# A transformer block on one core: gate rows in column groups, pool products in float32r passes, context keys with features on the partitions

## The chip, the cores and the metric

The kernel runs on one core of a Trainium2 chip. The metric is the time of one execution on the device in microseconds (us). The core has a TensorE (PE; its weight loads are shown apart as PEld), a VectorE (DVE), a ScalarE (ACT), a GpSimd (POOL) and a SyncE (SP), which here only issues transfers. All of them run side by side, each through its own list of instructions, and wait for one another on semaphores.

## What is computed

One layer of a diffusion backbone on 1024 latent tokens (a grid of 16 rows and 64 columns) and 256 context tokens, width 1024, in float32:

```
h_x = rmsnorm(x) * (1 + sc1) + sh1         # the same for the context, with its own shift and scale
u, q, k, v = split(h_x @ w_in)             # u: 512 wide for the pools; q, k, v: 8 heads of 64
pool:  y[g] = (window_mean(u[g], w) - u[g]) @ pool_w[g] * pool_scale     # 4 groups, w = 2, 4, 8, 16
attn:  softmax over an 8 x 16 neighbourhood (with a position bias) and all 256 context keys
x = x + gt1 * rmsnorm(concat(pool, attn) @ w_out)
x = x + gt2 * rmsnorm(relu(modulated(x) @ w_mlp_in) ** 2 @ w_mlp_out)
```

The shifts, scales and gates (sh, sc, gt) are six rows of `silu(c) @ w_mod + b_mod`, each 1024 long. Only the latent tokens are returned.

## The kernel before

**Number formats.** Most products are made of three float32r passes (helper `three`, L167 to L170): each operand is split into a high part (rounded to float32r) and a low part (the rest), and high x high, high x low and low x high are added up in PSUM. `split` (L142) makes the two parts: ScalarE casts the high one (L143), VectorE subtracts it from the source for the low one (L144). A few small products are plain float32 matmuls, which the trace shows as two records each: the sums of the modulation (L341), the gate rows (L198), the pools' products (L575), the scores (L669) and the weighted values (L745).

**Memory.** Large operands live in 33 equal pages of 128 x 1024 elements (`page`, pool "act", one tag). A page is given to a tile when its first instruction is issued, and goes back when the last instruction that reads it is done. Raw weights have 4 buffers (`wraw`), their high and low parts 8 (`whl`). During the projections PSUM has 6 banks for products (`ps1`) and 2 for lasting ones.

**Order.** In stretches marked `in_order` (the startup up to the context keys, the attention, the end of the MLP) each engine's instructions run in the order of the program. Elsewhere the framework that builds the kernel orders each engine's list: of the instructions whose inputs and buffers are free at that point, the one that stands first in the program is taken. The order is then fixed.

**The stages up to attention**, with what each leaves in pages:

1. Startup: tokens are normalised and transposed, `mod_rows` (L341) makes shift and scale with float32 products of 32 x 256 in four column groups of the array, keys kT are made for the latents (`some_keys`, L382). The modulated latents hx take 16 pages (2 blocks of 512 tokens, 8 k steps), kT takes 4.
2. Context keys (L494 to L517): `token_group` makes pkc, with tokens on the partitions, for two groups of 128 context tokens, 8 k steps of three passes of 512 columns each. ScalarE copies to kct; after each group of context values PE transposes four blocks of kct (L514) and ScalarE copies them to kcT, with the features on the partitions, which is what the scores need. The weights wv for the values take over the buffers of the key weights, and their splits stand after the second group (L501).
3. Values (pvc, pv; pages vc and v, 1 + 4). In between, VectorE does `background` steps: `mod_sum` (L190) adds 128 rows of w_mod at a time, weighted, into an accumulator of 128 x 1024 (accsh, accsc, acca, accb; b_mod is loaded into its first row). `mod_gate` (L193) sums an accumulator over the partitions, by a matmul with a matrix of ones, in two halves of 512 columns, and multiplies with the norm's gain; row 0 is stored to DRAM (L468) and read back as a page on all partitions when it is needed (L211): G1 near the end of attention, G2 in the MLP.
4. Pools (L581 to L588): for each of four groups, u is projected (two blocks of 512 tokens, pu), copied to a page u (L586), and `pooled` (L538) makes the window sums on VectorE in two pages sa and sb that take turns, then the difference from u; the page with the result is kept in dT.
5. Queries (L622): four groups for the first block of tokens, with background steps between them, the mask and the position tables (pages msk, U and four tab), one group for the second block, and `pool_out` (L571): one float32 product of 512 columns for each pool group and block, whose result is scaled and split into the page or raw buffer mix.
6. Attention, in 32 units, `in_order`: another query group, then for each unit scores, softmax, transposes and values. The last two query groups stand after the scores of units 0 and 1. VectorE adds the bias and takes the minimum (L683), ScalarE the exponential (L692).

After that come the output projection and the MLP (seven products in place of eight for each block, in `three` passes).

Of the kernel before, what the change touches and what calls it, by code (L numbers as in the profile page):

```python
# [10 lines left out]
F32 = mybir.dt.float32  # L11
F32R = mybir.dt.float32r
# [5 lines left out]
P = 128  # L18
D = 1024
KT = D // P  # L20
SEQ = 1024
NT = SEQ // P
CTX = 256
# [10 lines left out]
QR, QC = 16, 8  # L34
NM = GW // QC
# [44 lines left out]
def hybrid_block(ctx, tc, x, ctx_in, w_mod, b_mod, gp1, gp2, w_in, pool_w, rpb, w_out, w1, w2, vectors,  # L80
                 mask, edge, out):
    nc = tc.nc
    sub, mul, add = ALU.subtract, ALU.mult, ALU.add

    const = ctx.enter_context(tc.tile_pool(name="const", bufs=1))
    wraw = ctx.enter_context(tc.tile_pool(name="wraw", bufs=4))
# [11 lines left out]
    def page(name, dt=F32):  # L98
        return act.tile([P, 1024], dt, tag="pg", name=name)
# [21 lines left out]
    ident = cst("ident", [P, P])  # L121
    make_identity(nc, ident)
    ones = cst("ones", [P, P])
# [18 lines left out]
    def split(src, hi, lo):  # L142
        nc.scalar.copy(hi, src)  # L143
        nc.vector.tensor_tensor(lo, src, hi.bitcast(F32), sub)  # L144

    def load(name, src):
        raw = wraw.tile([P, 1024], F32, tag="raw", name=f"{name}w")
        nc.sync.dma_start(raw.rearrange("p (a b) -> p a b", b=src.shape[-1]), src)
        return raw
# [13 lines left out]
    def wk(w, k, lo, c, n):  # L163
        return w[k // 2][lo][:, (k % 2) * 512 + c : (k % 2) * 512 + c + n]


    def three(ps, ahi, alo, bhi, blo, first, last, more=False):  # L167
        nc.tensor.matmul(ps, ahi, bhi, start=first, stop=False, skip_group_check=more)  # L168
        nc.tensor.matmul(ps, ahi, blo, start=False, stop=False, skip_group_check=more)  # L169
        nc.tensor.matmul(ps, alo, bhi, start=False, stop=last, skip_group_check=more)  # L170
# [12 lines left out]
    def mod_sum(name, c, alloc, sT):  # L183
# [4 lines left out]
        for k in range(KT):  # L188
            w = load(f"wm{name}_{k}", w_mod[k * P : (k + 1) * P, c * D : (c + 1) * D])
            nc.vector.scalar_tensor_tensor(acc, w, sT[:, k : k + 1], acc, mul, add)  # L190
            yield acc

    def mod_gate(name, acc, gp, bank):  # L193
        g = load(f"gp{name}", gp.rearrange("(o d) -> o d", o=1).to_broadcast([P, D]).rearrange("p (a b) -> p a b", a=2))
        for h in range(2):
            hs = slice(h * 512, (h + 1) * 512)
            ps = bank(f"pg{name}{h}")
            nc.tensor.matmul(ps, ones, acc[:, hs], start=True, stop=True)  # L198
            nc.vector.tensor_tensor(acc[:, hs], ps, g[:, hs], mul)

    def mod_column(name, acc, bank):
        ps = bank(f"pc{name}")
# [4 lines left out]
    gates = {}  # L207
# [15 lines left out]
    with tc.tile_pool(name="ps1", bufs=6, space=PSUM) as ps1, tc.tile_pool(name="tmp1", bufs=3) as tmp:  # L223

        def bank(name):
            if name[:2] == "pm" or name in ("pxt0_6", "pxt0_7", "pxt1_6", "pxt1_7", "pct2", "pct3"):
                return lasting(name)
            return ps1.tile([P, 512], F32, tag="mm", name=name)

        def once(name, shape):  # L230
            return tmp.tile(shape, F32, tag=name, name=name, bufs=1)
# [141 lines left out]
        wgt = []  # L373
# [55 lines left out]
        for k in range(KT):  # L429
            for i in range(2):  # L430
                o = (k % 2) * 256 + i * P
                nc.tensor.transpose(pct[k // 2][:, o : o + P], cp[i][:, k * P : (k + 1) * P], ident)
        hc = []
        for k in range(KT):
            if k % 2 == 0:
                hp = page(f"hc{k}", F32R)
            o = (k % 2) * 512
# [23 lines left out]
        def mod_row(name, c, gp):  # L461
            for acc in mod_sum(name, c, page, sx):
                yield

            def close():
                mod_gate(name, acc, gp, bank)
                gates[name] = dram.tile([1, D], F32, tag=f"g{name}", name=f"g{name}")
                nc.sync.dma_start(gates[name], acc[0:1, :])  # L468

            closing.append(close)  # L470

# [14 lines left out]
        def token_group(ps, w, hk):  # L486
            for k in range(KT):
                hi, lo = hk(k)
                three(ps, hi, lo, wk(w, k, 0, 0, 512), wk(w, k, 1, 0, 512), k == 0, k == KT - 1)

        ctx_tok = lambda i: lambda k: (hc[k][0][:, i * P : (i + 1) * P], hc[k][1][:, i * P : (i + 1) * P])
        lat_tok = lambda b, i: lambda k: (hx[b][k][:, i * P : (i + 1) * P], hx[b][k][:, 512 + i * P : 512 + (i + 1) * P])

        kcp = page("kcT")  # L494
        kct = page("kct").rearrange("p (i f) -> p i f", i=2)
        raw_v = [load(f"wv{kk}", pair(w_in, kk, 1536, 512)) for kk in range(KT // 2)]
        for i in range(2):
            ps = bank(f"pkc{i}")
            token_group(ps, wgt, ctx_tok(i))
            if i:  # L500
                wgt = [high_low(f"wv{kk}", raw_v[kk]) for kk in range(KT // 2)]  # L501
            nc.scalar.copy(kct[:, i], ps)
        startup.close()
        with tc.issue_after(last[ET.DVE]):
            background(4)
# [1 line left out]
        for i in range(2):  # L507
            ps = bank(f"pvc{i}")
            token_group(ps, wgt, ctx_tok(i))
            nc.scalar.copy(vcp[:, i * 512 : (i + 1) * 512], ps)  # L510
            background()
            pt = bank(f"pkct{i}")
            for j in range(4):
                nc.tensor.transpose(pt[:, j * P : (j + 1) * P], kct[:, i, j * P : (j + 1) * P], ident)  # L514
            nc.scalar.copy(kcp.rearrange("p (j i t) -> p i j t", j=4, i=2)[:, i],
                               pt.rearrange("p (j t) -> p j t", j=4))
        kc = kcp.rearrange("p (j t) -> p j t", j=4)  # L517

        vp = [page(f"v{i}") for i in range(4)]
        for m in range(NM):  # L520
            ps = bank(f"pv{m}")
# [3 lines left out]
            if m == NM - 1:  # L525
                wgt = [high_low(f"wu{kk}", raw_u[kk]) for kk in range(KT // 2)]
# [4 lines left out]

        pwt = once("pwt", [P, 4, P])
        nc.sync.dma_start(pwt, pool_w.rearrange("g c d -> c g d"))
        edg = once("edg", [P, 4, 16])
        nc.sync.dma_start(edg, edge.rearrange("o (g e) -> o g e", g=4).to_broadcast([P, 4, 16]))
        dT = []

        def pooled(g, up):  # L538
            w = WINDOWS[g]
            lo, hi = w // 2, w - 1 - w // 2  # L540

            bufs = [page(f"sa{g}"), page(f"sb{g}")]
            cur, span, i = up, 1, 0
            while span < w:
                nxt = bufs[i % 2]
                i += 1
                n = SEQ - 2 * span + 1
                nc.vector.tensor_tensor(nxt[:, :n], cur[:, :n], cur[:, span : span + n], add)
                cur, span = nxt, 2 * span

            ed = tmp.tile([P, 16], F32, tag="ed", name=f"ed{g}", bufs=2)
            nc.vector.reduce_sum(ed[:, 0:1], up[:, 0 : hi + 1], axis=mybir.AxisListType.X)
            for q in range(1, lo):
                nc.vector.tensor_tensor(ed[:, q : q + 1], ed[:, q - 1 : q], up[:, hi + q : hi + q + 1], add)
            if hi:
                nc.vector.reduce_sum(ed[:, 7 + hi : 8 + hi], up[:, SEQ - 1 - lo : SEQ], axis=mybir.AxisListType.X)
            for q in range(hi - 2, -1, -1):
                t = SEQ - hi + q
                nc.vector.tensor_tensor(ed[:, 8 + q : 9 + q], ed[:, 9 + q : 10 + q], up[:, t - lo : t - lo + 1], add)
            dp = bufs[i % 2]  # L560
            nc.vector.scalar_tensor_tensor(dp[:, lo : SEQ - hi], cur[:, : SEQ - w + 1], 1.0 / w,
                                           up[:, lo : SEQ - hi], mul, sub)
            nc.vector.tensor_tensor(ed[:, :lo], ed[:, :lo], edg[:, g, :lo], mul)
            nc.vector.tensor_tensor(dp[:, :lo], ed[:, :lo], up[:, :lo], sub)
            if hi:
                nc.vector.tensor_tensor(ed[:, 8 : 8 + hi], ed[:, 8 : 8 + hi], edg[:, g, 8 : 8 + hi], mul)
                nc.vector.tensor_tensor(dp[:, SEQ - hi :], ed[:, 8 : 8 + hi], up[:, SEQ - hi :], sub)
            return dp


        def pool_out(g):  # L571
            dv = dT[g].rearrange("p (r m c) -> p m r c", r=QR, m=NM)
            for b in range(2):
                ps = bank(f"py{g}_{b}")
                nc.tensor.matmul(ps, pwt[:, g, :], dv[:, 4 * b : 4 * b + 4], start=True, stop=True)  # L575
                mp = page(f"mix1_{g}", F32R) if b else wraw.tile([P, 1024], F32R, tag="raw", name=f"mix0_{g}")
                nc.scalar.activation(mp[:, :512], ps, AF.Identity, scale=pscol[:, g : g + 1])
                nc.vector.scalar_tensor_tensor(mp[:, 512:], ps, pscol[:, g : g + 1], mp[:, :512].bitcast(F32), mul, sub)
                mix[b][g] = mp

        for g in range(4):  # L581
            up = page(f"u{g}")
            for b in range(2):
                ps = bank(f"pu{g}_{b}")
                feature_group(ps, wgt, g * P, b, range(KT))
                nc.scalar.copy(up.rearrange("p (r m c) -> p m r c", r=QR, m=NM)[:, 4 * b : 4 * b + 4],  # L586
                                   ps.rearrange("p (m r c) -> p m r c", m=4, r=QR))
            dT.append(pooled(g, up))  # L588


        tabs, msk = [], []
# [26 lines left out]
        wgt = in_group("wq", 512)  # L618
# [22 lines left out]
    with (  # L641
# [4 lines left out]
        bank = lasting  # L646
# [209 lines left out]
    with tc.tile_pool(name="ps2", bufs=6, space=PSUM) as ps2:  # L856
# [6 lines left out]
      with ExitStack() as tmp2:  # L863
        tmp = tmp2.enter_context(tc.tile_pool(name="tmp2", bufs=4))
# [342 lines left out]
        with tc.issue_after(first[ET.PE]), in_order(ET.PE, ET.Activation, ET.DVE, ET.SP):  # L1207
# [5 lines left out]
            tmp = tmp2.enter_context(tc.tile_pool(name="tmp3", bufs=4))  # L1213
# [138 lines left out]
```

## Time and profile before

| what | value |
|---|---|
| time, median of 3 runs | 1063.97 us (1063.96 to 1064.71) |
| the profiled execution | 1063.25 us |
| its span, first to last instruction | 1061.5 us |
| granted TensorE clock, mean | 0.997 |
| PE busy | 1045.0 us |
| VectorE / ScalarE busy | 685.6 / 506.8 us |
| context keys begin / values begin | 79.0 / 89.8 us |
| pools' projections | 148.9 to 192.4 us |
| first scores | 235.5 us |

How to read it: times in the trace are microseconds from the start of the span. A row of the timeline gives start, duration, engine, line, operation, output <- inputs, shape and count, and in brackets how long the engine was idle before and what it waited for. Buffer numbers are left out of names (pq0_1 is shown as pq). Matmuls are pipelined, so a record of a 512-column pass is 0.39 us long while the next one starts 0.23 us later: the spacing of the starts is what a pass costs. A float32 product has two records.

### The profile page before, as it was taken

To read this page: it belongs to the slowest core of one execution; us is meant where nothing else is said; L and a number is where in the kernel's file an instruction comes from. 1 tells how busy PE (TensorE), PEld (TensorE's weight loads), DVE (VectorE), ACT (ScalarE), POOL (GpSimd) and SP (SyncE) were. 2 spreads that over 40 slices of the span, in tenths; PEclk is the share of its full clock that TensorE was granted. 3 is DMA by queue.
4 is the path that set the end of the run, shared out by engine and by line. 5 is a ranking of instruction groups with operands and counts; after the bars stand their busy time and mean duration, and the time that the engine had idled before them with its cause. 6 is when DMAs were issued, how large, how long until landed. Compare 5 with 4: busy or idle time off the path is not lost.

```text
span 1061.5 us, 15251 instructions
## 1 busy us (share of the span) xinstructions
PE 1045.0 (98%) x5873; PEld 856.4 (81%) x5873; DVE 685.6 (65%) x1072; ACT 506.8 (48%) x881; POOL 55.7 (5%) x109
## 2 busy tenths in 40 slices
PE   7999999999999999999999999999999999999996
PEld 6788888867888888888888888888888888888885
DVE  6436634855999235799986666665577566557586
ACT  7554121235998123876555455554553335334441
POOL 2020000040120002200000000000000000000001
PEclk9999999999999999999999999999999999999998
DMA  9905740441111605445845445345597666546556
GB/s 343 324 21 198 243 174 0 138 134 40 42 41 47 174 1 171 145 149 183 259 168 175 140 138 190 129 151 196 209 355 253 243 238 220 192 164 205 173 188 206
DMA packets 94268, 179.37 MB, mean 169 GB/s; under 512 B 6898, under 2 KB 39154, under 8 KB 94196
## 3 DMA queue, kind: packets, MB, share of 16 engines
q1 hardware_dynamic: 76644, 144.80, 41.6%
q10 hardware_dynamic: 16272, 29.40, 7.5%
q0 software_dynamic: 1280, 4.21, 1.1%
q8 instruction: 46, 0.75, 0.3%
q14 instruction: 26, 0.21, 0.1%
HBM read 140.62 MB, written 37.76 MB: 168 GB/s over the span
## 4 chain that ended last, share of the span: by engine, by line
PE 89%; ACT 3%; DVE 3%; DMA 2%; SPq 1%; issue 1%; POOL 1%; POOLq 0%; DVEq 0%; ACTq 0%
PE pk L382 4%; PE S L669 3%; PE pa L745 3%; PE pyv L169 3%; PE pyv L168 3%; PE pyz L169 3%; PE pyz L168 3%; PE pyx L169 3%; PE phv L170 3%; PE phz L170 3%; PE pyx L170 3%; PE phz L168 3%; PE phv L168 3%; PE phv L169 3%; PE phz L169 3%; PE pyx L168 3%
## 5 line engine op out<-in xcount | busy, mean ns | idle before, releaser
L1001 ACT ACTIVATE c<-c 128x512 f32<-128x512 f32 x48 | 30.3, 632 | 60.4 <-DVE c L1114 23.8
L692 ACT ACTIVATE sp<-sp,nm 128x640 f32<-128x640 f32 (+1 forms) x64 | 51.3, 802 | 8.4 <-DVE nm L683 7.8
L683 DVE CUSTOM_DVE_ANT_0 sp<-S,tab 128x640 f32<-128x640 f32 (+1 forms) x56 | 42.8, 802 | 16.5 <-PE S L669 9.4
L144 DVE TENSOR_TENSOR wpS<-S,wpS 128x512 fp32r<-128x512 f32 x64 | 43.6, 686 | 11.8 <-ACT wpS L143 11.8
L168 PE MATMUL phx<-thB,wpA 128*128 128x512 f32 x128 | 49.9, 390 | 0.0
L170 PE MATMUL phx<-thB,wpA 128*128 128x512 f32 x128 | 49.9, 390 | 0.0
L169 PE MATMUL phx<-tlB,wpA 128*128 128x512 f32 x128 | 49.8, 389 | 0.0
L143 ACT CAST wpS<-S 128x512 fp32r<-128x512 f32 x64 | 39.2, 616 | 17.9 <-PE phy L170 7.5
L139 POOL TENSOR_TENSOR ry<-vy,nhalf 128x1 f32<-128x1 f32 x8 | 4.4, 550 | 600.7 <-DVE vy L137 600.7
L1002 ACT ACTIVATE c<-c 128x512 f32<-128x512 f32 x48 | 30.3, 631 | 8.0 <-DVE sa L1072 7.4
L1108 DVE TENSOR_TENSOR c<-phz,u 128x512 f32<-128x512 f32 x16 | 11.1, 691 | 32.2 <-PE phz L170 32.1
L669 PE MATMUL S<-kT,q 64*128 64x384 f32 (+1 forms) x128 | 27.9, 495 | 0.4 <-DVE nm L683 0.4
L170 PEld LDWEIGHTS phx<-thB,wpA 128*128 128x128 f32 x128 | 24.0, 188 | 5.2 <-DVE wpA L144 0.2
L169 PEld LDWEIGHTS phx<-tlB,wpA 128*128 128x128 f32 x128 | 24.0, 188 | 5.0
L168 PEld LDWEIGHTS phx<-thB,wpA 128*128 128x128 f32 x128 | 24.0, 188 | 4.9
L805 DVE TENSOR_TENSOR mp<-pw,Ga 128x512 f32<-128x512 f32 x14 | 9.6, 688 | 27.5 <-ACT jo L130 27.5
L745 PE MATMUL pa<-pt,v 128*64 128x128 f32 x352 | 25.9, 279 | 1.0 <-ACT px L725 0.3
L168 PE MATMUL phy<-thT,wpS 128*128 128x512 f32 x64 | 24.9, 389 | 0.0
L169 PE MATMUL phy<-tlT,wpS 128*128 128x512 f32 x64 | 24.9, 389 | 0.0
L170 PE MATMUL phy<-thT,wpS 128*128 128x512 f32 x64 | 24.9, 389 | 0.0
L168 PE MATMUL phz<-thT,wpS 128*128 128x512 f32 x64 | 24.9, 389 | 0.0
L169 PE MATMUL phz<-tlT,wpS 128*128 128x512 f32 x64 | 24.9, 389 | 0.0
(924 smaller groups left out, 3267.5 us busy)
## 6 DMA issues: line engine op xcount, KB each, us to landing
b<-in_w SPq DMA_DIRECT2D x64, 512.0 KB, 4.6
hrS<-hdS SPq DMA_DIRECT2D x32, 512.0 KB, 4.7
hrA<-hdA SPq DMA_DIRECT2D x24, 512.0 KB, 5.2
wm<-in_w_mod SPq DMA_DIRECT2D x16, 512.0 KB, 9.6
wa_0w<-in_w SPq DMA_DIRECT2D x16, 512.0 KB, 5.2
wa_1w<-in_w SPq DMA_DIRECT2D x16, 512.0 KB, 4.1
hdA<-c ACTq DMA_DIRECT2D x32, 256.0 KB, 2.3
hdS<-sa ACTq DMA_DIRECT2D x32, 256.0 KB, 4.3
```

Source lines behind the costliest of these rows:

```text
L143: nc.scalar.copy(hi, src)
L144: nc.vector.tensor_tensor(lo, src, hi.bitcast(F32), sub)
L168: nc.tensor.matmul(ps, ahi, bhi, start=first, stop=False, skip_group_check=more)
L169: nc.tensor.matmul(ps, ahi, blo, start=False, stop=False, skip_group_check=more)
L170: nc.tensor.matmul(ps, alo, bhi, start=False, stop=last, skip_group_check=more)
L382: nc.tensor.matmul(pks[b][j], wk(wgt, k, low, j * P, P), r, start=(k == 0 and n == 0), stop=(k == KT - 1 and n == 2))
L669: nc.tensor.matmul(S[e][:, c0 : c0 + keys.shape[1]], q[hs, cols], keys[hs], start=True, stop=True)
L683: nc.vector.tensor_tensor_reduce(out=to, in0=s, in1=bt, scale=1.0, scalar=BIG, op0=add, op1=ALU.min, accum_out=nm)
L692: nc.scalar.activation(sp, sp, AF.Exp, bias=least[i, e], scale=-1.0, accum_out=sums[i][:, e : e + 1])
L745: nc.tensor.matmul(pa[e * HD : (e + 1) * HD, cols], v[:, f : f + HD], turns[i][:, e, c] if c < 4 else fifths[i][:, :, (e + 1) * HD : (e + ...
L1001: nc.scalar.activation(r, src, AF.Relu)
L1002: nc.scalar.activation(r, r, AF.Square)
```

## The change

Three edits:

- `mod_gate`: the four quarters of a row (256 columns each) are summed by four matmuls with 32 columns of ones, each into its own 32 partitions of one PSUM bank. The gain is loaded by four transfers, a quarter onto 32 partitions each; VectorE makes one product of 256 columns; four transfers store the row.
- Context keys: for each of four feature groups j, the key weights (128 columns) are the stationary operand and the 256 context tokens the moving one, so the result has the features on the partitions and is copied straight into kcT. The transposes and the page kct go. The splits of wv stand after the fourth group.
- Pools: pool_w is split once into high and low parts (two buffers of 512 columns). The result of `pooled` is split for each block into a new page d{g}_{b} (high in its first half, low in its second), and `pool_out` makes three float32r passes from them.

```diff
@@ -190,13 +190,17 @@
             nc.vector.scalar_tensor_tensor(acc, w, sT[:, k : k + 1], acc, mul, add)
             yield acc
 
+
     def mod_gate(name, acc, gp, bank):
-        g = load(f"gp{name}", gp.rearrange("(o d) -> o d", o=1).to_broadcast([P, D]).rearrange("p (a b) -> p a b", a=2))
-        for h in range(2):
-            hs = slice(h * 512, (h + 1) * 512)
-            ps = bank(f"pg{name}{h}")
-            nc.tensor.matmul(ps, ones, acc[:, hs], start=True, stop=True)
-            nc.vector.tensor_tensor(acc[:, hs], ps, g[:, hs], mul)
+        g = wraw.tile([P, 1024], F32, tag="raw", name=f"gp{name}w")[:, :256]
+        quarters = gp.rearrange("(c o f) -> c o f", c=4, o=1)
+        for c in range(4):
+            nc.sync.dma_start(g[32 * c : 32 * c + 32, :], quarters[c].to_broadcast([32, 256]))
+        ps = bank(f"pg{name}")
+        for c in range(4):
+            nc.tensor.matmul(ps[32 * c : 32 * c + 32, :256], ones[:, :32], acc[:, c * 256 : (c + 1) * 256],
+                             start=True, stop=True)
+        nc.vector.tensor_tensor(acc[:, :256], ps[:, :256], g, mul)
 
     def mod_column(name, acc, bank):
         ps = bank(f"pc{name}")
@@ -465,7 +469,8 @@
             def close():
                 mod_gate(name, acc, gp, bank)
                 gates[name] = dram.tile([1, D], F32, tag=f"g{name}", name=f"g{name}")
-                nc.sync.dma_start(gates[name], acc[0:1, :])
+                for c in range(4):
+                    nc.sync.dma_start(gates[name][:, c * 256 : (c + 1) * 256], acc[32 * c : 32 * c + 1, :256])
 
             closing.append(close)
 
@@ -492,14 +497,15 @@
         lat_tok = lambda b, i: lambda k: (hx[b][k][:, i * P : (i + 1) * P], hx[b][k][:, 512 + i * P : 512 + (i + 1) * P])
 
         kcp = page("kcT")
-        kct = page("kct").rearrange("p (i f) -> p i f", i=2)
+        kc = kcp.rearrange("p (j t) -> p j t", j=4)
         raw_v = [load(f"wv{kk}", pair(w_in, kk, 1536, 512)) for kk in range(KT // 2)]
-        for i in range(2):
-            ps = bank(f"pkc{i}")
-            token_group(ps, wgt, ctx_tok(i))
-            if i:
+        for j in range(4):
+            ps = bank(f"pkc{j}")[:, :CTX]
+            for k in range(KT):
+                three(ps, wk(wgt, k, 0, j * P, P), wk(wgt, k, 1, j * P, P), *hc[k], k == 0, k == KT - 1)
+            if j == 3:
                 wgt = [high_low(f"wv{kk}", raw_v[kk]) for kk in range(KT // 2)]
-            nc.scalar.copy(kct[:, i], ps)
+            nc.scalar.copy(kc[:, j], ps)
         startup.close()
         with tc.issue_after(last[ET.DVE]):
             background(4)
@@ -509,12 +515,6 @@
             token_group(ps, wgt, ctx_tok(i))
             nc.scalar.copy(vcp[:, i * 512 : (i + 1) * 512], ps)
             background()
-            pt = bank(f"pkct{i}")
-            for j in range(4):
-                nc.tensor.transpose(pt[:, j * P : (j + 1) * P], kct[:, i, j * P : (j + 1) * P], ident)
-            nc.scalar.copy(kcp.rearrange("p (j i t) -> p i j t", j=4, i=2)[:, i],
-                               pt.rearrange("p (j t) -> p j t", j=4))
-        kc = kcp.rearrange("p (j t) -> p j t", j=4)
 
         vp = [page(f"v{i}") for i in range(4)]
         for m in range(NM):
@@ -531,6 +531,8 @@
 
         pwt = once("pwt", [P, 4, P])
         nc.sync.dma_start(pwt, pool_w.rearrange("g c d -> c g d"))
+        pwh, pwl = (tmp.tile([P, 512], F32R, tag=f"pw{n}", name=f"pw{n}", bufs=1) for n in "hl")
+        split(pwt.rearrange("p g d -> p (g d)"), pwh, pwl)
         edg = once("edg", [P, 4, 16])
         nc.sync.dma_start(edg, edge.rearrange("o (g e) -> o g e", g=4).to_broadcast([P, 4, 16]))
         dT = []
@@ -569,10 +571,11 @@
 
 
         def pool_out(g):
-            dv = dT[g].rearrange("p (r m c) -> p m r c", r=QR, m=NM)
             for b in range(2):
                 ps = bank(f"py{g}_{b}")
-                nc.tensor.matmul(ps, pwt[:, g, :], dv[:, 4 * b : 4 * b + 4], start=True, stop=True)
+                hi, lo = dT[g][b]
+                gs = slice(g * P, (g + 1) * P)
+                three(ps, pwh[:, gs], pwl[:, gs], hi, lo, True, True)
                 mp = page(f"mix1_{g}", F32R) if b else wraw.tile([P, 1024], F32R, tag="raw", name=f"mix0_{g}")
                 nc.scalar.activation(mp[:, :512], ps, AF.Identity, scale=pscol[:, g : g + 1])
                 nc.vector.scalar_tensor_tensor(mp[:, 512:], ps, pscol[:, g : g + 1], mp[:, :512].bitcast(F32), mul, sub)
@@ -585,7 +588,14 @@
                 feature_group(ps, wgt, g * P, b, range(KT))
                 nc.scalar.copy(up.rearrange("p (r m c) -> p m r c", r=QR, m=NM)[:, 4 * b : 4 * b + 4],
                                    ps.rearrange("p (m r c) -> p m r c", m=4, r=QR))
-            dT.append(pooled(g, up))
+            dv = pooled(g, up).rearrange("p (r m c) -> p m r c", r=QR, m=NM)
+            dT.append([])
+            for b in range(2):
+                d = page(f"d{g}_{b}", F32R)
+                hi, lo = d[:, :512], d[:, 512:]
+                bands = lambda t: t.rearrange("p (m r c) -> p m r c", m=4, r=QR)
+                split(dv[:, 4 * b : 4 * b + 4], bands(hi), bands(lo))
+                dT[g].append((hi, lo))
 
 
         tabs, msk = [], []
```

## The prediction

> **What bounds the kernel now.** I read the page first: busy times and the chain that ended last (part 4).
>
> ```profile
> span 1061.5 us, 15251 instructions
> PE 1045.0 (98%) x5873; PEld 856.4 (81%) x5873; DVE 685.6 (65%) x1072; ACT 506.8 (48%) x881; POOL 55.7 (5%) x109
> PE 89%; ACT 3%; DVE 3%; DMA 2%; SPq 1%; issue 1%; POOL 1%; POOLq 0%; DVEq 0%; ACTq 0%
> ```
>
> Then busy time by stretch (columns: PE, PEld, DVE, ACT, POOL, granted clock, DMA share, GB/s).
>
> ```profile
> 160.00:212.00 52.00, 52.00 (x227) 42.38 (x226) 33.03 (x63) 10.00 (x14) 1.44 (x2) 1.00 0.22 69
> 236.00:248.00 12.00, 12.00 (x60) 9.06 (x57) 3.19 (x10) 4.08 (x10) 0.00 (x0) 1.00 0.00 1
> 265.00:318.00 53.00, 52.28 (x816) 43.17 (x816) 49.29 (x146) 48.94 (x130) 10.45 (x24) 1.00 0.14 42
> 371.00:1000.00 629.00, 628.83 (x2808) 521.35 (x2807) 421.90 (x539) 309.48 (x469) 14.40 (x24) 1.00 0.55 186
> ```
>
> PE is the bound in the projections and in the MLP (628.83 of 629 us); in attention PE, VectorE and ScalarE are all near full. So time taken from PE before attention comes off the end, and a late attention start is not won back. The chain over the stretch of the change (start, us, what) shows its PE work on the path:
>
> ```profile
> 208.91 1.72 PE pga L198 x4
> 221.55 1.72 PE pgb L198 x4
> 223.27 6.87 PE py L575 x16
> ```
>
> **Gate rows.** Each gate is now two float32 products of 512 columns, 1.72 us. Mod_rows already runs float32 products of 256 columns in four column groups:
>
> ```profile
> 50.18 1.93 PE L341 MATMUL pm<-wm,sT 128*32 128x256 f32 x32
> 52.05 1.20 PE L382 MATMUL pk<-hx,wk2h 128*128 128x512 f32 x4
> ```
>
> Two records make a product, so 16 products took 52.05 - 50.18 = 1.87 us, 0.47 us for four, changes of tile shape included. A gate falls from 1.72 to 0.47: -1.25, twice, **-2.5**. Bounds: 0 if the groups don't overlap (then the change doesn't do what it says), -2.6 if four cost a fourth of 1.72. VectorE has one product of 256 columns for two of 512. SP issues four loads and four stores for one each; the gates are read only when attention ends and in the MLP, so SP's extra microseconds fall on gate loads that have slack.
>
> **Context keys.** 48 passes of 512 columns become 96 of 256, each with its own weight load; eight transposes go.
>
> ```profile
> 78.96 0.39 PE L168 MATMUL pkc<-wk0h,hc 128*128 128x512 f32 x1
> 89.84 0.39 PE L168 MATMUL pvc<-wv0h,hc 128*128 128x512 f32 x1
> 95.06 0.39 PE L170 MATMUL pvc<-wv3h,hc 128*128 128x512 f32 x1
> 95.95 0.39 PE L169 MATMUL pvc<-wv0l,hc 128*128 128x512 f32 x1
> ```
>
> The passes take (89.84 - 78.96)/48 = 0.227 us each. [...] For 256 columns I take 0.107 + 0.012 = 0.12: 96 x 0.12 = 11.5 against 10.9, +0.6. Between the last two rows lie one pass more and four transposes: 0.89 - 2 x 0.227 = 0.43, twice, -0.86. Bounds of a short pass: 0.113 (half of 0.227), and a load that doesn't hide:
>
> ```profile
> L204 PE MATMUL pcsh<-ones,accsh x16: 164/250/250, 112.6 to 114.2; 128*128 128x1 f32 x16
> ```
>
> One column with a load takes 1.6/15 = 0.107, so load plus stream would be 0.214: 96 x 0.214 = 20.5, +9.7, less the transposes +8.8. [...] The splits of wv now follow the fourth group:
>
> ```profile
> 85.74 1.05 ACT L143 CAST wv0h<-wv0w 128x1024 fp32r<-128x1024 f32 x1 [0.54 <-PE pkc L169]
> 86.82 1.22 DVE L144 TENSOR_TENSOR wv0l<-wv0w,wv0h 128x1024 fp32r<-128x1024 f32 x1 [5.28 <-ACT wv0h L143]
> ```
>
> wk0's buffers come free 0.7 us into a 2.9 us group, at 88.4; 1.1 and 1.2 us later, at 90.7, wv0l is ready, and PE wants it at 90.6. Cost 0.2. Context keys together: **-0.1**, from -0.9 to +9.
>
> [...]
>
> **Pools' products.** 24 float32r passes x 0.227 = 5.44 for 6.87: **-1.4**; the form is that of the projections' passes, so no bound is needed. Added: one split of pwt and eight of half a page, of the size of these on the page:
>
> ```profile
> L144 DVE TENSOR_TENSOR wpS<-S,wpS 128x512 fp32r<-128x512 f32 x64 | 43.6, 686 | 11.8 <-ACT wpS L143 11.8
> L143 ACT CAST wpS<-S 128x512 fp32r<-128x512 f32 x64 | 39.2, 616 | 17.9 <-PE phy L170 7.5
> ```
>
> That is 9 x 0.62 = 5.6 us on ScalarE and 9 x 0.69 = 6.2 on VectorE. By themselves they cost nothing: ScalarE worked 10 and VectorE 33 of the 52 us from 160 to 212. So **PE alone gives -4.0**: 1063.25 - 4.0 = 1059.2.
>
> **The pages.** The splits also need pages, and there are 33. During the pools 27 are held: hx 16, kT 4, kcT, vc, v 4, acca. Six are left for u, sa, sb and the kept results. That these six are used up now is visible:
>
> ```profile
> 197.63 0.39 PE L170 MATMUL pq<-hx,wq3l 128*128 128x512 f32 x1
> 202.10 0.60 ACT L628 ACTIVATE q<-pq 128x512 f32<-128x512 f32 x1 [8.17 <-DVE ed L559]
> 208.51 0.40 PE L170 MATMUL pq<-hx,wq3l 128*128 128x512 f32 x1
> 211.36 0.60 ACT L628 ACTIVATE q<-pq 128x512 f32<-128x512 f32 x1 [7.26 <-PE pq L170]
> 213.45 0.31 POOL L600 MEMSET tab<- 128x256 f32 x1 [0.37 <-PE pq L170]
> 214.13 0.31 POOL L600 MEMSET tab<- 128x256 f32 x1 [0.37 <-PE pq L170]
> ```
>
> The first query sum is done at 197.9 but kept at 202.1, when VectorE is through with pools page sb3. The third is done at 208.7 and kept at 211.4, when the fourth group has read hx0_0 for the last time; the tables get a page each 0.68 us, one k step. Kept now are three pages (dT0 to 2) beside u3, sa3, sb3: six. After the change each group keeps two (d{g}_0, d{g}_1). Group 2 then needs four kept, u2, sa2 and sb2: **seven**. sb2 has no page at 183.6. Nothing frees one before the fourth query group, which frees hx0; acca waits for its gate, which stands after the third. Behind sb2 on VectorE stand the rest of group 2, its splits and all of group 3, and pool_out waits for those; on ScalarE u3 waits too, and behind it the queries' copies. accb can't have a page either, so VectorE has nothing else to go on with but wq's splits and acca's last step. PE goes on: pu3 twice, pq0, pq1, pq2 and pga fill the six PSUM banks exactly, and the fourth query group waits some 0.7 us for pga's product.
>
> ```profile
> 208.74 1.88 PE L198 MATMUL pga<-acca,ones 128*128 128x512 f32 x4
> 183.62 1.22 DVE L548 TENSOR_TENSOR sb<-sa 128x1021 f32<-128x1021 f32 x1
> 187.53 0.16 DVE L567 TENSOR_TENSOR sb<-ed,u 128x3 f32<-128x3 f32 x1
> 187.84 0.16 DVE L552 TENSOR_REDUCE ed<-u 128x1 f32<-128x8 f32 x1
> 189.40 0.17 DVE L563 TENSOR_TENSOR ed<-ed,edg 128x8 f32<-128x8 f32 x1
> 194.62 1.22 DVE L548 TENSOR_TENSOR sa<-u 128x1023 f32<-128x1023 f32 x1
> 195.83 1.27 DVE L190 SCALAR_TENSOR_TENSOR acca<-wma_7w,sx,acca 128x1024 f32<-128x1024 f32 x1
> 202.67 0.17 DVE L567 TENSOR_TENSOR sa<-ed,u 128x7 f32<-128x7 f32 x1
> 206.15 1.28 DVE L190 SCALAR_TENSOR_TENSOR accb<-wmb_0w,sx,accb 128x1024 f32<-128x1024 f32 x1 [3.31 <-DMA accb<-in_b_mod]
> ```
>
> (The row at 195.83 also shows that VectorE's order isn't the program's: that step comes from the queries, and was put between two of group 3 because it was ready.) So pq3 begins at 208.74 + 0.47 + 0.65 = 209.9, frees hx0_0 at 210.8, and VectorE then has before it: the rest of group 2, 183.62 to 187.69, 4.1; u3's edges, 187.84 to 189.57, 1.7; group 3, 194.62 to 202.84 less acca's 1.2, 7.0; four low halves at 0.69, 2.8; accb's eight steps of 1.3 (it gets its page late too), 10.6; gate b 0.4 (an estimate, half of a product of 512 columns and a little); and the pools' low halves, eight of the row below at 0.8 with its gap, 6.6. That is 33.2 us from 210.8: **244.0**.
>
> ```profile
> L578 DVE SCALAR_TENSOR_TENSOR mix<-py,cols,mix x8: 749/750/752, 224.9 to 230.9; 128x512 fp32r<-128x512 f32 x8
> 235.52 0.70 PE L669 MATMUL S<-kcT,q 64*128 64x256 f32 x4
> 236.69 0.69 DVE L683 CUSTOM_DVE_ANT_1 sp<-S,tab 128x512 f32<-128x512 f32 x1 [5.04 <-PE S L669]
> 242.25 0.92 PE L669 MATMUL S<-kT,q 64*128 64x384 f32 x4
> ```
>
> The first scores stand at 235.52, a query group covers VectorE's work on them, and the second scores at 242.25 need that work done. If the first scores get their banks early, the second start when two of the row at 236.69 are done, at 244.0 + 1.5 = 245.5, **+3.3**. If they wait for the last pool bank, they start at 244.0, **+8.5**. Banks are given back one by one by the low halves that come last in the backlog, so I take the middle, **+6**; the -4.0 on PE is inside it, since VectorE sets the start. 1063.25 + 6 = 1069.3. The median of the runs shown, 1063.97, is 0.7 above the profiled execution; measurement here tells about 0.2% (2 us) from no change.
>
> **The rivals.**
> 1. *The pages don't bind* (another page comes free early, or the splits are ordered later). For it: VectorE has 19 us idle in 160 to 212. Against it: the two waits above. PE's sum holds: 1059.2. This is the faster side; it decides if sb2 is written before 190.
> 2. *They bind, but the backlog is absorbed*: accb's 10.6 us are done in the gaps of 236 to 248, where VectorE works 3.2 of 12 us. Then 22.6 us of backlog end at 233.4, 2 us ahead of the 235.5 of now, and 10.6 - 8.8 = 1.8 don't fit into the gaps: about 0, 1063. Against it: accb stands before the scores in the program, and its page comes at 212, so its steps are ready first.
> 3. *The short passes don't hide their loads*: +8.8 on PE ahead of all that, 1078.
> 4. *Worse starvation*: the tables and the mask, which now get their pages from hx0 (rows at 213.45 and 214.13), take them while VectorE is busy, and sb3 waits until pool_out has read d0 at 221.5 instead of 217.5: 4 us more, 1073.
>
> [...]
>
> **How the numbers follow.** Forecast 0.58, with its two ends 1066.5 and 1072 as its own range; rival 1 0.20; rival 2 0.10; rival 3 0.04; rival 4 0.08. Faster: rival 1 and the lower part of rival 2, 0.24; the same 0.06; slower 0.70. The range reaches down to rival 1, 1059, since without it 0.2 and more would be left out, and up to 1075, past rival 4; rival 3 and the low tail of rival 1 are left out, some 0.15.
>
> **What would show it.** sb2's first write at 210 and not 183; pu3 kept by ScalarE some 24 us after its sum; PE idle before pq3 and before the first or second scores; gate products of 0.5 us; pkc passes 0.12 apart; py in 5.4 us. Wrong if sb2 is on time or the second scores start by 242.

## The result

The changed kernel takes **1112.3 us** (median of four runs, 1111.3 to 1113.5) against 1064.0 us for the kernel before (1063.8 to 1064.7): a ratio of 1.0455, 95% interval 1.0442 to 1.0469. The prediction said 1069.3, and at most 1075. The profiled execution of the changed kernel took 1113.17 us; its page begins so (span; busy time by engine; the chain that ended last, by engine):

```profile
span 1111.4 us, 15408 instructions
PE 1046.9 (94%) x5929; PEld 862.3 (78%) x5929; DVE 688.8 (62%) x1079; ACT 509.2 (46%) x890; POOL 55.7 (5%) x109
PE 84%; ACT 4%; DVE 4%; SPq 3%; issue 3%; DMA 1%; POOL 1%; DVEq 0%; POOLq 0%; ACTq 0%
```

Busy times of all engines are those of before to within 6 us, while the span is 49.9 us longer. So hardly any work was added: engines stood still. To find where, I set the start of each stage on PE beside that of before:

| first instruction of | before, us | after, us | later by, us |
|---|---|---|---|
| mod products `pm` | 20.0 | 54.9 | 34.9 |
| context keys `pkc` | 79.0 | 112.5 | 33.5 |
| pools `pu` | 148.9 | 182.4 | 33.5 |
| gate a `pga` | 208.7 | 242.3 | 33.6 |
| gate b `pgb` | 221.4 | 272.5 | 51.1 |
| first scores `S` | 235.5 | 283.7 | 48.2 |
| second scores | 242.3 | 292.1 | 49.8 |
| w_out products `phx` | 439.9 | 489.8 | 49.9 |

The loss lies in two places: 33.5 us ahead of the context keys, and 16.3 us between gate a and the second scores. These are the profiled executions, whose spans are 49.9 us apart; the medians are 48.3 apart, so by them the second loss is nearer 48.3 - 33.5 = 14.8. The first loss is nowhere in the prediction; the second is its page term, which it had at 6.

**The first place.** The timeline of the changed kernel around it (start, us; duration; engine; line; what; in brackets the idle time before and what ended it):

```profile
13.56 0.19 ACT L130 ACTIVATION_READ_ACCUMULATOR jkx<-x 128x1 f32 x1
46.94 0.62 ACT L143 CAST pwh<-pwt 128x512 fp32r<-128x512 f32 x1 [33.19 <-DMA pwt<-in_pool_w]
47.46 1.05 ACT L130 ACTIVATE jkx<-x 128x1024 f32<-128x1024 f32 x1
48.64 0.15 DVE L135 TENSOR_SCALAR vt_x<-ms_x 128x1 f32<-128x1 f32 x1 [33.45 <-ACT jkx L130]
50.13 4.80 PE L300 MATMUL pxt<-ident,x 128*128 128x128 f32 x30 [34.55 <-DVE xT L307]
35.69 2.45 SPq L249 DMA_DIRECT2D c<-in_ctx  x2
38.18 0.43 SPq L533 DMA_DIRECT2D pwt<-in_pool_w  x1
```

In the timeline of before, the eighth square is done and the first mod product starts here:

```profile
14.65 0.18 ACT L130 ACTIVATION_READ_ACCUMULATOR jkx<-x 128x1 f32 x1
19.96 2.19 PE L341 MATMUL pm<-wm,sT 128*32 128x256 f32 x32
```

The cast of `pwt`, the high half of the pools' weights, is written at L535, behind the context values. In ScalarE's list it stands between the seventh and the eighth square of x. There it waits 33.19 us for pwt's transfer, which SP issues at 38.18, behind the loads of the mod weights and of the context. The eighth square waits behind it, VectorE waits for that square, PE for VectorE. The startup's `in_order` ties the startup's own instructions to one another; it does not keep others out. So in that stretch an engine's list is not simply the order of the program, as the section on the kernel before has it.

**The second place**, in the same timeline:

```profile
215.85 1.23 DVE L550 TENSOR_TENSOR sa<-u 128x1023 f32<-128x1023 f32 x1 [4.19 <-ACT u L589]
243.03 0.42 DVE L203 TENSOR_TENSOR acca<-pga,gpaw 128x256 f32<-128x256 f32 x1 [13.63 <-PE pga L201]
244.60 1.23 DVE L550 TENSOR_TENSOR sb<-sa 128x1021 f32<-128x1021 f32 x1 [1.14 <-PE pq L170]
249.54 1.07 ACT L589 COPY u<-pu 128x512 f32<-128x512 f32 x2
248.73 0.96 POOL L185 MEMSET accb<- 128x1024 f32 x1 [141.32 <-PE pq L170]
258.33 1.29 DVE L144 TENSOR_TENSOR d<-sa,d 128x512 fp32r<-128x512 f32 x2 [0.47 <-ACT d L143]
259.54 1.28 DVE L190 SCALAR_TENSOR_TENSOR accb<-wmb_0w,sx,accb 128x1024 f32<-128x1024 f32 x1
271.13 1.28 DVE L190 SCALAR_TENSOR_TENSOR accb<-wmb_7w,sx,accb 128x1024 f32<-128x1024 f32 x1
272.52 1.08 PE L201 MATMUL pgb<-accb,ones 128*32 128x256 f32 x8 [12.76 <-issue]
283.74 0.70 PE L679 MATMUL S<-kcT,q 64*128 64x256 f32 x4 [2.34 <-DVE mix L581]
292.06 0.92 PE L679 MATMUL S<-kT,q 64*128 64x384 f32 x4
```

Read from the top: `sa` of pools group 2 is written at 215.85, `sb` only at 244.60, when the fourth query group has read the first page of hx. Less the 33.5 us that the startup lost, that is 211.1; the prediction said 210.8. Group 3 ends at 259.5. Only then do the eight steps of accb run, and gate b on PE waits for them: 12.76 us without work. All the pools' products and both scores stand behind gate b in PE's list.

### The profile page after: what moved, and what is told of

Same layout as the page of the kernel before. It is cut to its first block, busy times and chain, and to the rows that moved or that the text cites. A ratio compares the mean times of both kernels' runs of the same rounds, so it can differ in the third digit from the quotient of the medians.

```text
span 1111.4 us, 15408 instructions
## 1 busy us (share of the span) xinstructions
PE 1046.9 (94%) x5929; PEld 862.3 (78%) x5929; DVE 688.8 (62%) x1079; ACT 509.2 (46%) x890; POOL 55.7 (5%) x109
## 4 chain that ended last, share of the span: by engine, by line
PE 84%; ACT 4%; DVE 4%; SPq 3%; issue 3%; DMA 1%; POOL 1%; DVEq 0%; POOLq 0%; ACTq 0%
PE pk L386 4%; PE S L679 3%; PE pa L755 3%; PE pyv L170 3%; PE pyz L170 3%; PE pyx L168 3%; PE phv L169 3%; PE phz L169 3%; PE pyv L168 3%; PE pyz L168 3%; PE phv L168 3%; PE phz L168 3%; PE pyx L170 3%; PE pyx L169 3%; PE phv L170 3%; PE phz L170 3%
## 5 line engine op out<-in xcount | busy, mean ns | idle before, releaser
L170 PE MATMUL phx<-thB,wpA 128*128 128x512 f32 x128 | 49.9, 390 | 0.1
L168 PE MATMUL phx<-thB,wpA 128*128 128x512 f32 x128 | 49.9, 390 | 0.0
L169 PE MATMUL phx<-tlB,wpA 128*128 128x512 f32 x128 | 49.8, 389 | 0.0
L300 PE MATMUL pxt<-ident,x 128*128 128x128 f32 x64 | 9.8, 307 | 38.0 <-DVE xT L307 35.9
L300 PEld LDWEIGHTS pxt<-ident,x 128*128 128x128 f32 x64 | 8.3, 159 | 39.5 <-DVE xT L307 36.4
L1118 DVE TENSOR_TENSOR c<-phz,u 128x512 f32<-128x512 f32 x16 | 11.1, 691 | 32.3 <-PE phz L170 32.1
L168 PE MATMUL phy<-thT,wpS 128*128 128x512 f32 x64 | 24.9, 389 | 0.0
L169 PE MATMUL phy<-tlT,wpS 128*128 128x512 f32 x64 | 24.9, 389 | 0.0
L170 PE MATMUL phy<-thT,wpS 128*128 128x512 f32 x64 | 24.9, 389 | 0.0
```

## The theories

**A.** The startup's loss is the place of pwt's cast in ScalarE's list, in front of a late transfer, and nothing else. Rival: the new buffers or a new order of the loads delay the startup.
**B.** The second loss comes from the want of pages: sb2 has none, then accb has none. Rival: the eight new splits are themselves too much work for VectorE there.
**C.** Most of it is accb's lateness, because gate b stands ahead of the pools' products in PE's list. Rival: PE would wait for group 3 as long anyway.
**D.** Gates and context keys are worth on PE what the prediction said. Rivals: VectorE sets the start of attention in any case; short passes don't hide their weight loads.

| kernel | time, us (lowest to highest) | ratio to before, 95% interval |
|---|---|---|
| split_alone | 1097.4 (1097.2 to 1097.5) | 1.0316 [1.0301, 1.0330] |
| late_split | 1078.3 (1077.4 to 1079.2) | 1.0138 [1.0121, 1.0155] |
| early_load | 1081.6 (one run) | |
| own_accb | 1066.8 (1066.2 to 1067.8) | 1.0028 [1.0018, 1.0038] |
| halves_at_use | 1063.2 (1062.6 to 1065.4) | 0.9998 [0.9989, 1.0007] |
| two_more | 1070.1 (1068.8 to 1071.3) | 1.0058 [1.0043, 1.0073] |
| pages_32 | 1068.1 (1067.7 to 1069.7) | 1.0044 [1.0027, 1.0060] |
| gates_only | 1061.8 (1061.5 to 1062.5) | 0.9981 [0.9972, 0.9990] |
| gates_keys | 1061.8 (1061.4 to 1062.5) | 0.9980 [0.9971, 0.9989] |
| pools_at_use | 1064.4 (1063.9 to 1065.7) | 1.0006 [0.9998, 1.0015] |

## Experiments on the startup

**late_split**: the changed kernel, with the split of pwt held behind what ScalarE and VectorE issued last in the startup.

```
-        split(pwt.rearrange("p g d -> p (g d)"), pwh, pwl)
+        with tc.issue_after(last[ET.Activation]), tc.issue_after(last[ET.DVE]):
+            split(pwt.rearrange("p g d -> p (g d)"), pwh, pwl)
```

> Theory A: the cast of pool_w stands in ScalarE's list inside the startup, ahead of the eighth square, and waits there for a transfer that SP issues only at 38 us; that is 33.4 us of the 49.9 by which the span grew. With the split behind the startup the first product of mod_rows is back at 20 us and the profiled execution takes 1113.2 - 33.4 = 1079.8 us (1078 to 1081.5). Rival: the transfers of the startup or PE's low clock there took the time and the cast only shows it; then the wait moves to the next instruction that needs late data and the time stays above 1105. The 16.3 us between the pools and the second scores stay in both.

Measured: 1078.3, 34 us less than the changed kernel. The first mod product starts at 20.1, the context keys at 79.2. The view of tile pwt shows the cast where nobody waits for it:

```profile
L143 ACT CAST pwh<-pwt x1: 622/622/622, 92.7 to 92.7; 128x512 fp32r<-128x512 f32 x1
```

**split_alone**: the kernel before, with only the split of pwt added where the change has it. Nothing reads the halves, and the pools' products stay as they were.

> The kernel before with nothing added but the split of pwt, where the change puts it; its halves are read by nobody and the pools' products stay as before. Theory (the cast of pwt is put among the startup's squares on ScalarE and waits there for pwt's transfer): the whole startup loss of the change is here, the first mod product at 53 to 55 us instead of 20.0, and about +33 us, 1097. Rival (the startup is late because of the new page and buffer use, or of the new order of the other loads): no loss, 1064 to 1065.

Measured: 1097.4, +33.4. Two instructions and one wait cost as much as the changed kernel loses in the startup. Its timeline has them:

```profile
46.68 0.62 ACT L143 CAST pwh<-pwt 128x512 fp32r<-128x512 f32 x1 [33.17 <-DMA pwt<-in_pool_w]
49.87 5.24 PE L296 MATMUL pxt<-ident,x 128*128 128x128 f32 x30 [34.54 <-DVE xT L303]
```

A holds, and the rival falls: this kernel has no new page, and SP issues its loads in the order of before. The two new buffers for the halves are there, but late_split has them too, without the loss.

**early_load**: the changed kernel, with pwt loaded by ScalarE's queue right behind the first vectors, and the split left where it was.

```
         nc.scalar.dma_start(cols, vectors)
+        pwt = once("pwt", [P, 4, P])
+        nc.scalar.dma_start(pwt, pool_w.rearrange("g c d -> c g d"))
...
-        pwt = once("pwt", [P, 4, P])
-        nc.sync.dma_start(pwt, pool_w.rearrange("g c d -> c g d"))
```

> The split of pool_w keeps its place in the startup, but its transfer is issued by ScalarE right behind that of the vectors. Theory A (only the wait for the transfer costs): 1080 us (1078.5 to 1082), the startup longer than in the kernel before by no more than the 0.6 us of the cast and the 0.7 us of the low half. Rival: the place of the split itself disturbs the order of the startup; then 1090 us or more.

Measured: 1081.6 (one run); mod products at 24.9, context keys at 82.5. The time lies in the range expected, but not for the reason given: the startup was to be longer by at most 1.3 us, and 4.9 stay at the mod products, 3.5 at the context keys. The cast moved too. In this kernel's timeline it stands ahead of the first square and waits there:

```profile
10.53 0.62 ACT L143 CAST pwh<-pwt 128x512 fp32r<-128x512 f32 x1 [5.43 <-DMA pwt<-in_pool_w]
```

SP waited for the same transfer, 4.8 us, and issued the first weight load at 10.53 (at 5.31 in late_split), so this run doesn't tell apart what the cast's place and what SP's wait cost. The earlier load left a part of the loss; holding the split back left none.

## Experiments on the pages

In late_split the startup is as before, so the second loss stands alone: 1078.3 - 1063.8 = 14.5 us. Its timeline has the marks of the changed kernel, on the clock of before:

```profile
211.24 1.22 DVE L551 TENSOR_TENSOR sb<-sa 128x1021 f32<-128x1021 f32 x1 [1.14 <-PE pq L170]
236.23 1.28 DVE L190 SCALAR_TENSOR_TENSOR accb<-wmb_7w,sx,accb 128x1024 f32<-128x1024 f32 x1 [0.17 <-DMA wmb_7w<-in_w_mod]
237.61 1.08 PE L201 MATMUL pgb<-accb,ones 128*32 128x256 f32 x8 [11.20 <-issue]
248.01 1.23 PE L680 MATMUL S<-kcT,q 64*128 64x256 f32 x4 [2.61 <-DVE mix L582]
256.21 0.92 PE L680 MATMUL S<-kT,q 64*128 64x384 f32 x4
```

**halves_at_use**: late_split, but a group keeps its one page until pool_out, and the halves are made there in two buffers of their own. The same splits, no page more than before.

```
...
+                d = tmp.tile([P, 1024], F32R, tag="d", name=f"d{g}_{b}", bufs=2)
+                hi, lo = d[:, :512], d[:, 512:]
+                split(dv[:, 4 * b : 4 * b + 4], bands(hi), bands(lo))
...
-                hi, lo = dT[g][b]
...
-            dv = pooled(g, up).rearrange("p (r m c) -> p m r c", r=QR, m=NM)
...
+            dT.append(pooled(g, up))
```

> The split of pool_w behind the startup, and the pools' results split only in pool_out, in two buffers of their own, so that each group keeps one page as before; the same 8 casts and 8 low halves are done. Theory B (pages): sb of the third group is written at 183.6 as before, and the 16.3 us go: 1060 to 1063 us, the sum on PE (-4.0) less up to 3 us of waiting where two buffers take turns. Rival: the 16.3 us come from the added work on ScalarE and VectorE, or from the transfers of the gates on SP; then 1075 to 1081.

Measured: 1063.2, the time of before (0.9998, 0.9989 to 1.0007) and just above the range expected. The 14.5 us go with the pages, while the split work stays, though at another place; two_more and pages_32 below leave that place as it is.

**own_accb**: late_split, with accb in a buffer of its own instead of a page; the pages stay short for the pools.

```
-            for acc in mod_sum(name, c, page, sx):
+            for acc in mod_sum(name, c, page if name == "a" else lambda n: once(n, [P, D]), sx):
```

> The split of pool_w behind the startup, the pools' pages as in the change, but the accumulator of gate b in a buffer of its own. Theory C: of the 16.3 us, 8 to 11 are accb's eight steps and gate b, which have no page until the fourth query group and which PE's list puts ahead of the pools' products; they are now done while the pools' chain is blocked: 1069 to 1072 us. Rival: the blocked chain of the third and fourth pool group alone sets the start of the scores: 1077 to 1081.

Measured: 1066.8, 11.5 us less than late_split and 2 us below the range expected. The timeline shows accb's steps in the gap in which VectorE had nothing to do, and gate b no longer waits:

```profile
197.43 1.28 DVE L190 SCALAR_TENSOR_TENSOR accb<-wmb_0w,sx,accb 128x1024 f32<-128x1024 f32 x1 [1.32 <-DMA wmb_0w<-in_w_mod]
210.98 1.28 DVE L190 SCALAR_TENSOR_TENSOR accb<-wmb_7w,sx,accb 128x1024 f32<-128x1024 f32 x1 [1.05 <-DMA wmb_7w<-in_w_mod]
213.65 1.22 DVE L551 TENSOR_TENSOR sb<-sa 128x1021 f32<-128x1021 f32 x1 [1.05 <-PE pq L170]
224.89 0.64 PE L201 MATMUL pgb<-accb,ones 128*32 128x256 f32 x8
236.53 0.70 PE L680 MATMUL S<-kcT,q 64*128 64x256 f32 x4 [1.88 <-DVE mix L582]
244.84 0.92 PE L680 MATMUL S<-kT,q 64*128 64x384 f32 x4
```

sb2 is as late as before the edit, even 2.4 us later, and still most of the loss is gone. So C holds: of the 14.5 us, 11.5 go with accb's page. Of the 3.0 that stay, not all is shown to be sb2's lateness: the first scores are 1.0 us later than in before, the second 2.6, and the 1.6 between them come with a lower clock, 0.50 from 238 to 240 (see the last section).

**two_more**: late_split, with the halves of group 0 in two buffers of their own, which leaves two pages more.

```
-                d = page(f"d{g}_{b}", F32R)
+                d = (tmp.tile([P, 1024], F32R, tag="d", name=f"d{g}_{b}", bufs=2) if g == 0
+                     else page(f"d{g}_{b}", F32R))
```

> late_split, but with the halves of group 0 in two buffers of their own, so that two pages more are there; the arithmetic is the same. Theory (pages): sb2 is written on time at 184, the block moves on to sb3, which waits until 211; 5.8 us of group 3, 1.3 of its low halves and accb's 10.5 end at 230, and gate b starts there instead of at 237.6: 1069 to 1071 against 1078.3 of late_split. Rival (VectorE's added work as such sets the start of gate b): nothing, 1078.

Measured: 1070.1. The block has moved from group 2 to group 3, and gate b starts at 230.4, where the page theory put it. From its timeline:

```profile
210.87 1.23 DVE L551 TENSOR_TENSOR sb<-sa 128x1021 f32<-128x1021 f32 x1 [0.44 <-PE pq L170]
230.40 1.08 PE L201 MATMUL pgb<-accb,ones 128*32 128x256 f32 x8 [3.90 <-issue]
```

**pages_32**: the kernel before, with 32 pages instead of 33 and nothing of the change.

```
-    act = ctx.enter_context(tc.tile_pool(name="act", bufs=33))
+    act = ctx.enter_context(tc.tile_pool(name="act", bufs=32))
```

> The kernel before with 32 pages instead of 33; the arithmetic and every instruction are the same. Theory (the want of pages delays VectorE, and PE stands at gate b): five are left for the pools, so group 3's second page sb3 waits until the fourth query group has read hx0 for the last time, 211 instead of 197.0; its 5.8 us and accb's eight steps of 1.3 with their gaps end at 228, gate b starts 6 us late, and with PE at a lower clock behind the wait 1069 to 1072. Rival (the splits' own work or their place in the order makes the loss, and not the pages): 1064.

Measured: 1068.1, +4.1, a us below what was expected. One page fewer makes the same stall without a single new instruction: sb of group 3 at 211.69 instead of 197.02, gate b at 229.84 instead of 221.4. From its timeline:

```profile
211.69 1.23 DVE L548 TENSOR_TENSOR sb<-sa 128x1021 f32<-128x1021 f32 x1
229.84 1.98 PE L198 MATMUL pgb<-accb,ones 128*128 128x512 f32 x4 [2.53 <-DVE accb L190]
```

B holds.

## Experiments on the parts

**gates_only** is the kernel before with the diff's hunks of `mod_gate` and of the gates' stores; **gates_keys** has the hunks of `kcp` beside them; **pools_at_use** is the kernel before with the pools' hunks as in halves_at_use and the split of pwt as in late_split.

> The kernel before with the gate rows in four column groups and nothing else. Theory (PE sets the start of attention in the kernel before, so what is taken from PE ahead of it comes off the end): two gates at 0.57 instead of 1.72 us, -2.3 us, 1061.7. Rival (VectorE sets the start of attention in any case, as it does where the pools' halves are made at their use): nothing, 1064.

Measured: 1061.8, -2.2 (0.9972 to 0.9990). Gate a takes 0.57 us of PE and the first scores start 1.5 us earlier, with no wait ahead of them, in PE's timeline:

```profile
209.02 0.64 PE L200 MATMUL pga<-acca,ones 128*32 128x256 f32 x8
233.99 0.70 PE L673 MATMUL S<-kcT,q 64*128 64x256 f32 x4
```

> The kernel before with the gate rows and the context keys of the change, without the pools' products. Theory (both are PE's time, and PE sets the end): gates -2.3; keys 11.6 us for 96 passes instead of 10.9 for 48 and the transposes gone, together +0.7 - 0.6 = about 0; so 1061.5 to 1062, with the gates' share. Rival (the passes of 256 columns don't hide their weight loads): +8.8 on the keys, 1070. Rival (VectorE sets the start of attention): 1064.

Measured: 1061.8, the same as gates_only. So the context keys are worth nothing. In the changed kernel's timeline of PE they are 96 passes in 124.08 - 112.50 = 11.58 us:

```profile
112.50 0.28 PE L168 MATMUL pkc<-hc,wk0h 128*128 128x256 f32 x1
112.61 0.28 PE L169 MATMUL pkc<-hc,wk0h 128*128 128x256 f32 x1
124.08 0.39 PE L168 MATMUL pvc<-wv0h,hc 128*128 128x512 f32 x1
```

That is 0.12 each, +0.7 beside the 48 passes of before; the context values then take 135.2 - 124.1 = 11.1 instead of 101.5 - 89.8 = 11.7, -0.6.

> The kernel before with the pools' products in three passes, their halves made at the use and the split of pwt behind the startup; gates and keys as before. Theory (PE's 24 passes are 1.4 us shorter, but the eight low halves and the copies out of PSUM then fall on VectorE within the same 14 us and set the start of attention): +1 to +2 us, 1065 to 1066. Rival (the halves are free as the prediction had it): -1.4, 1062.6.

Measured: 1064.4, ratio 1.0006 (0.9998 to 1.0015): no gain, and less loss than expected. The window from 222 to 236 of this kernel (columns: PE, PEld, VectorE, ScalarE, POOL, clock, DMA share, GB/s) and the first scores, in its timeline, show why:

```profile
222.00:236.00 14.00, 13.71 (x53) 9.00 (x51) 10.49 (x16) 9.31 (x16) 5.23 (x14) 1.00 0.16 41
```

```profile
236.58 0.70 PE L677 MATMUL S<-kcT,q 64*128 64x256 f32 x4 [0.88 <-DVE mix L586]
```

PE's passes are shorter, but the start of the scores is set by VectorE, which has the low halves of d and of mix, 10.49 of 14 us, in a chain with ScalarE's casts.

gates_only and gates_keys are some 0.2% faster than the kernel before, with intervals clear of 1; nothing is gained by adding the pools' products (halves_at_use, 1063.2).

## Why the prediction was wrong

- **"By themselves they cost nothing"** is the step that failed worst, 33.4 of 48.3 us. It priced the split of pwt at 0.62 + 0.69 us, and looked for cover where the line stands in the program. Its place in the engine's list was never asked for, nor when its input arrives. Both could have been: the prediction itself noted that VectorE's order isn't the program's, and the trace of before shows in its view of tile pwt that a load written at L533 goes out in the startup, and late:

```profile
L533 SPq DMA_DIRECT2D pwt<-in_pool_w x1: 432/432/432, 38.9 to 38.9; - x1
DMA to landing us min/median/max: 8.8/8.8/8.8
```

  38.9 + 8.8 = 47.7: there, nothing that reads pwt can run earlier, nor can what stands behind it in an engine's list (in the changed kernel the cast ran at 46.94, the eighth square behind it at 47.46). Against the squares of x, done by 14.8 in before, that row gives 33 us for a cast that is put ahead of one of them. No rival named it, so the range couldn't hold it.
- **"So I take the middle, +6"**: the mechanism was right, sb2 at 210.8 (211.2 in late_split), accb behind group 3, its last step due at 244.0 - 0.4 - 6.6 = 237.0 (measured 236.23 + 1.28 = 237.5). From there it took 7.0 us to the first scores; late_split took 10.5. The sum let the pools' low halves run as if their products were there. But gate b and py stand in PE's list behind accb, so PE's passes, at a clock of 0.50 until 240.9, and ScalarE's copies came first.
- **The lower end of that term** let the first scores start early and put the second 1.5 us behind the backlog. But the scores stand behind py on PE, and the second a whole query group later: 242.25 - 235.52 = 6.7 us in before, 256.21 - 248.01 = 8.2 in late_split. So the upper end, the first scores behind the last pool bank, was the case: +8.5 as worked out; in late_split +12.5 at the first scores and +14.5 in the time. In the changed kernel's profiled execution it was +16.3, where VectorE waited 2.09 us for one of accb's weights as well.
- **PE alone gives -4.0**: gates -2.5, measured -2.2; a gate takes 0.57, not 0.47. Context keys -0.1, measured 0.0. No run shows the two parts of that term's pass, 0.107 us for streaming 256 columns (used in rival 3's +8.8 too) and 0.012 on top; the changed kernel showed the whole pass, 11.58/96 = 0.121 us. Pools' products -1.4: lost, +0.4 (-0.2 to +1.6), since even without the want of pages VectorE sets the first scores.
- **Rival 1** (pages don't bind) is refuted by the wait of sb2, and would hardly have given 1059.2 either: halves_at_use, where no page is wanting, took 1063.2. **Rival 2** (accb absorbed in later gaps) is refuted by PE's wait ahead of gate b, 11.20 us in late_split: PE needs accb before py and the scores. **Rival 3** (loads not hidden) is refuted by 0.12 per pass: 96 passes with as many loads took 11.6 us, not the 20.5 that the prediction worked out for loads in full. **Rival 4** (sb3 late) did not show: in late_split group 3 follows group 2 without a gap over 1 us.
- **The signs** named in advance came: sb2's time, pu3's two halves kept 29 and 24 us after their sums, PE idle before the first scores (2.34 us), gate products near 0.5, short passes 0.12 apart. Two did not: py took 281.2 - 273.5 = 7.7 us instead of 5.4, and PE had no long wait before pq3 but one of 12.76 ahead of gate b.

## What to carry to other kernels

Where a framework orders the engines' lists, a new instruction's place is not its line: ask first when its input lands, and what stands behind it if it is put as early as possible, then hold it back if that is long. When a pool of buffers runs out, follow the want to the last tile that asks for one, and to the instruction that stands first on the bounding engine and needs it; here that tile, accb, made 11.5 of the 14.5 us. A shorter pass was worth its length here only where its engine set the next start: gates_only took 2.2 us less, pools_at_use 0.4 more.

## What the runs showed of the chip

The granted clock fell with PE's waits. While PE waited for gate b in the changed kernel it was 1.00 from 260 to 264, 0.62 from 264 to 266 and 0.50 from 266 on, and it stayed at 0.50 behind the wait, to 278. In that kernel's windows around gate b (columns as above) and in its timeline of PE:

```profile
260.00:273.00 13.00, 0.48 (x8) 0.23 (x8) 9.82 (x8) 0.77 (x2) 0.00 (x0) 0.67 0.49 171
273.00:284.00 11.00, 8.66 (x34) 6.29 (x28) 5.88 (x9) 5.82 (x10) 3.99 (x10) 0.77 0.26 61
```

```profile
275.40 0.63 PE L169 MATMUL py<-d,pwh 128*128 128x512 f32 x1
275.83 0.63 PE L170 MATMUL py<-d,pwl 128*128 128x512 f32 x1
278.50 0.39 PE L168 MATMUL py<-d,pwh 128*128 128x512 f32 x1
278.73 0.40 PE L169 MATMUL py<-d,pwh 128*128 128x512 f32 x1
```

The passes of py are 0.43 us apart until 278.0 and 0.23 from then on. After 3.90 us without work (two_more) they were 0.43 apart too, to 236.3, and the clock from 232 to 236 was 0.50. The slow stretch behind the wait for gate b was 5.5 us in the changed kernel (272.5 to 278.0), 5.9 in two_more and 3.3 in late_split, so its length varies.

Shorter waits, ahead of the first scores, were followed by a stretch at a clock of 0.50 too: 1.88 us (own_accb), 2.34 (the changed kernel, 0.50 from 285 to 288), 2.58 (early_load) and 2.61 (late_split). Others had none: 1.57 us ahead of the first scores of pages_32, 1.72 in two_more, and 2.53 ahead of gate b in pages_32, where the clock stayed at 1.00. So the length of the one wait alone doesn't decide here; what does was not shown.

At the scores the price can be read. From the first to the second, PE has the same work: 6.7 us in before, two_more and pages_32, and 8.2 to 8.3 in the four kernels with a slow stretch there, 1.5 to 1.6 us more. What the slow stretch behind gate b costs in the end is not measured by itself: py takes 7.7 us instead of 5.4 in the changed kernel, but PE then waits for VectorE in any case.
